# A decoder layer's up projection: the first two column pairs as plain products, the combinations of X on VectorE, and another order of the loads of h

## The chip, the cores and the metric

The kernel runs on one core of a Trainium2 chip. The metric is the device time of one execution in microseconds (us); of several runs the median is given.

## What is computed

One step of a one-layer decoder on 1056 rows: 32 sample rows (8 sequences of 4) and 1024 prompt rows, each 1024 wide. Attention, retention, their merge and the output projection come first. The change concerns what follows them, the convolutional feed-forward part, cut from the reference:

```
def conv_ffn(xn, conv_ctx, w_up, conv_w, conv_b, w_down):
    T = xn.shape[1]
    u = xn @ w_up
    u_ext = jnp.concatenate([conv_ctx.astype(u.dtype), u], axis=1)
    c = conv_b
    for tap in range(CONV_W):
        c = c + u_ext[:, tap:tap + T] * conv_w[tap]
    a, b = jnp.split(c, 2, axis=-1)
    h = jax.nn.gelu(a, approximate=True) * b
    return h @ w_down, u_ext[:, -(CONV_W - 1):]
```

w_up is 1024 x 6144, w_down 3072 x 1024. All values are float32.

## The kernel before, in words

**Precision.** Every float32 operand is kept as two parts, hi and lo. A product takes three matmuls: hi by hi, hi of the weight by lo of X, lo of the weight by hi of X (`mm3`, lines 238, 239, 240). `split` makes the parts: ScalarE casts hi (line 215), and `ew` subtracts it from the source to get lo, on VectorE (line 210) or GpSimd (line 212), as its first argument says. `V`, `G`, `S` and `TE` are VectorE, GpSimd, ScalarE and TensorE.

**Layout.** X, the normed input of the feed-forward part, lies transposed: 8 chunks of 128 features by 1056 columns (rows of the step). The columns are cut into four quarters of HW = 264, called (j, half): j = 0, 1 and half = 0, 1. A matmul here is 128 x 128 weights by 128 x 264 columns.

**Pairs.** w_up is worked through in 24 pairs of one gate block and one linear block of 128 columns each. A plain pair takes 8 chunk products for each of 2 blocks and 4 quarters, 192 matmuls: that is `eight`, used for pair 0. The other pairs use `pair(i)`, a Strassen-like scheme with seven products (A11, A12, A22, S1 to S4) instead of eight for each j, 168 matmuls. It needs sums of the four 128x512 parts of the weights (`up_weights`, on GpSimd), their hi and lo (`w_split`), and sums of quarters of X: `combos(j, ...)` makes t0, t1 and t2, `extra` splits three of them into the tiles ex40, ex50, ex20 (j = 0) and ex41, ex51, ex21 (j = 1), which serve the products S2, S3 and A22, and `t1` with `to_b12` writes one combination over a quarter of X itself. These combinations are made once and then serve all pairs. Part of this work is on GpSimd: the `ew(G, ...)` in `combos`, two instructions in `extra` (lines 911 and 912), and `t1(0, tmp, G)`.

**Pair 1 before.** It has an order of products of its own (`head`): A11, A12, S2, S3, S1, A22, S4. Its results are added to each other on VectorE as they come (lines 990 to 1012; line 1003 adds S1's, 998 and 999 add A11's to those of S2 and S3 in the usual order).

**Convolution and h.** After each pair, `conv` makes three taps on ScalarE and VectorE (lines 1052 to 1056), the gelu (1059), the product of both halves (a `ew` on c_out), and stores that block of h to HBM from GpSimd's queue (line 1062).

**Loads of h.** The down projection reads h back as two hi and lo parts. `load_h(0, n, ...)` loads n = 0 to 11 for j = 0: q = n % 6 takes four blocks of h (three for q = 5 at j = 0, whose fourth comes from SBUF), n // 6 is the half. So n = 5 and n = 11 need the h of pair 22, the others that of earlier pairs. The loads are issued during the last pair, two after each product, in the order 0 to 11, from GpSimd's queue (line 1035), into three buffers (`hrp`); each is then split into a place that the last pair no longer needs. For j = 0, n odd and below 6 the lo part is made on GpSimd. TensorE's first run through the down projection takes them in the order (0, q = 0 to 4), (1, q = 0 to 3), (0, 5), (1, 4), (1, 5), written (half, q), that is n = 0 to 4, 6 to 9, 5, 10, 11; each is 12 matmuls.

**What sets the order.** The code gives data and engines; the framework's scheduler places the instructions of each engine in a fixed order by its own model. So instructions of one pair, the conv of the one before and the combinations interleave, and an instruction waits for those in front of it on its engine even where its own data is ready.

Of the kernel before, what the change touches and what calls it, by code (L numbers as in the profile page):

```python
# [8 lines left out]
F32 = mybir.dt.float32  # L9
# [8 lines left out]
P = 128  # L18
# [6 lines left out]
T = NS + SEQ  # L25
# [94 lines left out]
def trunk(ctx, tc, I, O):  # L120
# [691 lines left out]
    def quad(j, r, half, a, b):  # L812
        c = (2 * j + half) * HW
        return [f32(x)[:, 4 * r:4 * r + 4, c + a:c + b] for x in X]

    def combos(j, a, b):
        b11, b12, b21, b22 = (quad(j, r, half, a, b) for r in range(2) for half in range(2))
        if j not in raws:
            raws[j] = [tr.tile([P, 4, HW], F32, name="t%d" % q) for q in range(3)]
        t2, t3, t = [x[:, :, a:b] for x in raws[j]]  # L820
        ew(V, t3, b22[0], b12[0], sub)
        ew(G, t, b22[1], b12[1], sub)
        ew(V, t3, t3, t, add)
# [83 lines left out]
    def extra(j, a, b):  # L907

        t2, t3, t = [x[:, :, a:b] for x in raws[j]]
        b21 = quad(j, 1, 0, a, b)  # L910
        G.tensor_tensor(out=t, in0=b21[0], in1=t2, op=sub)
        G.tensor_tensor(out=t, in0=t, in1=b21[1], op=add)
        for p, src in ((S2, t2), (S3, t3), (A22, t)):
            split(ex[p, j][:, 0, :, a:b], ex[p, j][:, 1, :, a:b], src)

# [48 lines left out]
    def pair(i):  # L964

        ws = up_weights(i)
        u, us = u_tile(i)
        banks, u3s, ts = {}, {}, {}
        head = i == 1

        def bank(j, b):
            if (j, b) not in banks:
                banks[j, b] = ps_8(j)
            return banks[j, b][:, :HW]

        def product(p, j, t):
            b, first = {A11: (0, True), A12: (0, False), S2: (1, True), S3: (1, False),
                        S1: (2, True), S4: (2, False), A22: (3, True)}[p]
            ps = bank(j, b)
            for k in range(4):  # L980
                xh, xl = xop(p, j, k)
                mm3(ps, t[:, k], t[:, 4 + k], xh, xl, first and k == 0, k == 3,
                    skip_group_check=not first)
            c12, c22 = u_dst(u, 0, j, 1), u_dst(u, 1, j, 1)
            if p == S3:
                u3s[j] = u3p.tile([P, HW], F32, name="u3")
            if p == A11 and head:
                S.copy(out=c22, in_=ps)
            elif p == S2 and head:
                V.tensor_tensor(out=c12, in0=ps, in1=c22, op=add)  # L990
            elif p == S3 and head:
                V.tensor_tensor(out=u3s[j], in0=ps, in1=c22, op=add)
            elif p == S2:
# [12 lines left out]
            if p == (A22 if head else A11):
                ps, u3 = bank(j, 3), u3s[j]
                if j == 0:
                    V.tensor_tensor(out=us[:, 1, :, 2:6], in0=smp(ps[:, :NS]), in1=smp(u3[:, :NS]),
                                    op=add)  # L1010
                    ps, u3 = ps[:, NS:], u3[:, NS:]
                V.tensor_tensor(out=u_dst(u, 1, j, 0), in0=ps, in1=u3, op=add)

        for p in (A11, A12, S2, S3, S1, A22, S4) if head else (S2, A22, S3, A11, S1, A12, S4):
            t = w_split(ws[p], G if p in (S3, A12) and not head else V)
            for j in range(2):
                product(p, j, t)
            if i == NPAIR - 1:
                hs.extend([load_h(0, len(hs) + e, slot(p, e)) for e in range(2 if p != S4 else 0)])
        return u, us  # L1020


# [7 lines left out]
    def load_h(j, n, sl):  # L1030

        q, c = n % 6, (2 * j + n // 6) * HW
        nk = 3 if j == 0 and q == 5 else 4
        raw = hrp.tile([P, 4, HW], F32, name="h_raw")[:, :nk]
        HL.dma_start(out=raw, in_=h_d[4 * q:4 * q + nk, :, c:c + HW].rearrange("k p c -> p k c"))
        put_h(sl, slice(0, nk), raw, G if HG(j, n) else V)
        return sl

    def put_h(sl, ks, src, eng=None):
# [26 lines left out]
    tmp = fup.tile([P, 2, UW], F32, name="u_ext").rearrange("p g x -> p (g x)")[:, :4 * HW]
    tmp = tmp.rearrange("p (k x) -> p k x", k=4)
    u, us = u_tile(0)
    wp = [wcols(w_up, g * NPAIR * P, P) for g in range(2)]

    def eight(j):
        for half in range(2):
            for g in range(2):
                ps = gemm_chunk(wp[g], actX, (2 * j + half) * HW, HW, ps=ps_8())
                evict(u, us, g, j, half, ps)

    eight(0)
    extra(0, 0, HW)
    t1(0, tmp, G)
    to_b12(0, tmp)  # L1080
    eight(1)
    combos(1, 0, J1B)
    combos(1, J1B, HW)
    extra(1, 0, HW)
    t1(1, raws[1][1], V)
    to_b12(1, raws[1][1])
    tr_stack.close()
    fp = pool("fp", 1, stack=fr_stack)
    hrp = pool("hrp", 3, stack=fr_stack)
    hs, HL = [], st  # L1090

    def HG(j, n):
        return j == 0 and n < 6 and n % 2 == 1

    conv(0, u, us)
    for i in range(1, NPAIR):
        u, us = pair(i)
        hlast = conv(i, u, us)
    for n in (5, 11):
# [41 lines left out]
    for j in range(2):  # L1141
        facc, nxt = [], []
        for m in range(KD):
            f = fd.tile([P, 2 * HW], F32, name="facc%d" % m)
            facc.append(f)
            last = m == KD - 1
            wts = [wcols(w_down, m * P, P, q3 * D) for q3 in range(3)]
            if j == 0 and m == 0:
                runs = [(0, q) for q in range(5)] + [(1, q) for q in range(4)] + [(0, 5), (1, 4), (1, 5)]
            elif m == 0 or last:  # L1150
                runs = [(half, q) for half in range(2) for q in range(6)]
            else:
                runs = [(half, 2 * q3 + e) for q3 in range(3) for half in range(2) for e in range(2)]
            pss = [ps_8()[:, :HW] for half in range(2)]
            if last and j == 1:
                break
            for n, (half, q) in enumerate(runs):
                wh, wl = wts[q // 2]
                for k in range(4):
                    hh, hl = (t[:, k] for t in hs[6 * half + q])  # L1160
                    kk = 4 * (q % 2) + k
                    mm3(pss[half], wh[:, kk], wl[:, kk], hh, hl, q == 0 and k == 0, q == 5 and k == 3)
                if q == 5:
                    S.copy(out=f[:, half * HW:half * HW + HW], in_=pss[half])
                if last:
                    if n < 6:
                        nxt.append(load_h(1, n, hs[n]))
                    elif n < 8:
                        nxt.append(load_h(1, n, FREE[n - 6]))
                        FREE.append(hs[n])  # L1170
                    else:
                        FREE.append(hs[n])
                        nxt.append(load_h(1, n, FREE[n - 6]))
        if j == 0:
            for r0, n in DROWS:
                final(0, r0, n)
            hs = nxt
    for half, c, w, rws in DLAST:
        ps = pss[0] if half == 0 else ps_8()[:, :w]
        for q in range(6):  # L1180
# [65 lines left out]
```

## Time and profile before

| what | value |
|---|---|
| median of 3 runs | 1760.26 us (1759.06 to 1760.69) |
| the profiled execution, its own time | 1756.41 us |
| its span, first to last instruction | 1754.6 us |
| TensorE busy | 1712.9 us (98%) |
| VectorE, ScalarE, GpSimd busy | 1081.6, 699.8, 455.5 us |
| mean granted TensorE clock | 0.995 |
| first matmul of the up projection, of the last pair | at 931.01, at 1418.82 us of the span |

The span is shorter than the execution's own time, since it counts from the first to the last instruction. A matmul's row shows some 0.28 us, though the next begins 0.12 us after it: they overlap in the pipeline, so the distance of their starts is their price. PE is TensorE, DVE VectorE, ACT ScalarE, POOL GpSimd; PEclk is the granted clock as a share of full speed.

### The profile page before, as it was taken

To read this page: it belongs to the slowest core of one execution; us is meant where nothing else is said; L and a number is where in the kernel's file an instruction comes from. 1 tells how busy PE (TensorE), PEld (TensorE's weight loads), DVE (VectorE), ACT (ScalarE), POOL (GpSimd) and SP (SyncE) were. 2 spreads that over 40 slices of the span, in tenths; PEclk is the share of its full clock that TensorE was granted. 3 is DMA by queue.
4 is the path that set the end of the run, shared out by engine and by line. 5 is a ranking of instruction groups with operands and counts; after the bars stand their busy time and mean duration, and the time that the engine had idled before them with its cause. 6 is when DMAs were issued, how large, how long until landed. Compare 5 with 4: busy or idle time off the path is not lost.

```text
span 1754.6 us, 31005 instructions
## 1 busy us (share of the span) xinstructions
PE 1712.9 (98%) x12513; PEld 1680.3 (96%) x12513; DVE 1081.6 (62%) x2084; ACT 699.8 (40%) x1464; POOL 455.5 (26%) x575
## 2 busy tenths in 40 slices
PE   6999999999999999999999899999999999999997
PEld 6999999999999999999789799999999999999997
DVE  6889654438484846545457987777777784127213
ACT  5544433224242435513324545444454553225222
POOL 4111111001111111000135765555545561003001
PEclk9999999999999999999999999999999999999999
DMA  8223234622222232443321122323222246338332
GB/s 226 62 80 94 70 115 145 209 73 62 91 63 89 64 106 71 172 133 100 102 85 66 50 90 88 96 73 95 89 74 74 82 144 209 97 95 273 105 97 76
DMA packets 196064, 183.60 MB, mean 105 GB/s; under 512 B 16208, under 2 KB 173552, under 8 KB 195904
## 3 DMA queue, kind: packets, MB, share of 16 engines
q1 hardware_dynamic: 180320, 128.46, 24.6%
q0 software_dynamic: 15600, 53.15, 8.6%
q8 instruction: 98, 1.61, 0.4%
q14 instruction: 46, 0.38, 0.1%
HBM read 137.87 MB, written 43.68 MB: 103 GB/s over the span
## 4 chain that ended last, share of the span: by engine, by line
PE 82%; issue 9%; DVE 4%; DMA 2%; POOL 1%; ACT 1%; SPq 1%; POOLq 0%; DVEq 0%; ACTq 0%
PE ps_mm L238 12%; PE ps_mm L239 12%; PE ps_mm L240 12%; PE ps_m L240 8%; PE ps_m L238 8%; PE ps_m L239 8%; PE ps_t L238 4%; PE ps_t L240 4%; PE ps_t L239 4%; DMA h_raw<-h_d 1%; PE ps_a L446 1%; PE ps_c L481 1%; DVE ex L210 1%; PE ps_b L469 1%; DVE t L210 0%
## 5 line engine op out<-in xcount | busy, mean ns | idle before, releaser
L238 PE MATMUL ps_mm<-xh,w_hi 128*128 128x384 f32 (+1 forms) x1080 | 354.7, 329 | 0.0
L239 PE MATMUL ps_mm<-xl,w_hi 128*128 128x384 f32 (+1 forms) x1080 | 352.9, 327 | 0.8 <-DVE xl L210 0.8
L240 PE MATMUL ps_mm<-xh,w_lo 128*128 128x384 f32 (+1 forms) x1080 | 351.5, 326 | 0.0
L210 DVE SCALAR_TENSOR_TENSOR w_lo<-w_raw,w_hi 128x1024 fp32r<-128x1024 f32 x107 | 130.7, 1222 | 231.2 <-ACT w_hi L229 231.0
L229 ACT CAST w_hi<-w_raw 128x1024 fp32r<-128x1024 f32 x108 | 113.3, 1049 | 282.4 <-PE ps_m L239 134.9
L239 PEld LDWEIGHTS ps_mm<-xl,w_hi 128*128 128x128 f32 x1080 | 204.0, 189 | 1.9 <-DVE xl L210 1.1
L238 PEld LDWEIGHTS ps_mm<-xh,w_hi 128*128 128x128 f32 x1080 | 204.1, 189 | 1.3 <-issue 1.0
L240 PEld LDWEIGHTS ps_mm<-xh,w_lo 128*128 128x128 f32 x1080 | 204.0, 189 | 0.7 <-issue 0.7
L1056 DVE SCALAR_TENSOR_TENSOR c_out<-u_ext,fconst,c_out 128x1024 f32<-128x1024 f32 x96 | 129.4, 1349 | 38.1 <-ACT c_out L1052 37.9
L265 POOL TENSOR_TENSOR rs<-ms,mhalf 128x1 f32<-128x1 f32 (+2 forms) x73 | 50.8, 697 | 367.9 <-DVE ms L263 255.1
L238 PE MATMUL ps_m<-xh,w_hi 128*128 128x264 f32 (+2 forms) x472 | 134.8, 286 | 2.7 <-ACT xh L215 2.7
L239 PE MATMUL ps_m<-xl,w_hi 128*128 128x264 f32 (+2 forms) x472 | 135.1, 287 | 0.7 <-DVE xl L210 0.6
L240 PE MATMUL ps_m<-xh,w_lo 128*128 128x264 f32 (+2 forms) x472 | 134.6, 285 | 0.0
L238 PE MATMUL ps_m<-xh,w 128*128 128x264 f32 x368 | 105.6, 287 | 8.8 <-DVE u_ext L1003 6.5
L238 PE MATMUL ps_m<-ex,w_hi 128*128 128x264 f32 x384 | 109.1, 284 | 0.9 <-ACT w_hi L229 0.9
L240 PE MATMUL ps_m<-ex,w_lo 128*128 128x264 f32 x384 | 109.4, 285 | 0.5 <-DVE w_lo L210 0.5
L239 PE MATMUL ps_m<-ex,w_hi 128*128 128x264 f32 x384 | 108.8, 283 | 0.0
L238 PE MATMUL ps_t<-xh,w 128*128 128x264 f32 x368 | 104.9, 285 | 0.8 <-DVE u_ext L1003 0.4
L240 PE MATMUL ps_m<-xh,w 128*128 128x264 f32 x368 | 105.2, 286 | 0.0
L239 PE MATMUL ps_m<-xl,w 128*128 128x264 f32 x368 | 105.1, 286 | 0.0
L239 PE MATMUL ps_t<-xl,w 128*128 128x264 f32 x368 | 104.7, 284 | 0.0
L240 PE MATMUL ps_t<-xh,w 128*128 128x264 f32 x368 | 104.3, 283 | 0.0
(384 smaller groups left out, 4903.6 us busy)
## 6 DMA issues: line engine op xcount, KB each, us to landing
w_raw<-in_w_up SPq DMA_DIRECT2D x48, 512.0 KB, 3.9
w_raw<-in_w_down SPq DMA_DIRECT2D x48, 512.0 KB, 3.9
w_raw<-in_w_in SPq DMA_DIRECT2D x42, 512.0 KB, 4.0
h_d<-c_out POOLq DMA_DIRECT2D x24, 528.0 KB, 3.0
h_raw<-h_d POOLq DMA_DIRECT2D x22, 528.0 KB, 5.2
xt<-in_x_prompt SPq DMA_DIRECT2D x16, 512.0 KB, 4.4
gm_d<-gstage POOLq DMA_DIRECT2D x22, 192.0 KB, 2.2
gm<-gm_d SPq DMA_DIRECT2D x8, 528.0 KB, 4.1
```

The costliest lines, as they stand in the source:

```text
L210: V.scalar_tensor_tensor(out=out, in0=in0, scalar=1.0, in1=in1, op0=mult, op1=op)
L229: S.copy(out=hi, in_=raw)
L238: TE.matmul(ps, wh, xh, start=start, stop=False, **kw)
L239: TE.matmul(ps, wh, xl, start=False, stop=False, **kw)
L240: TE.matmul(ps, wl, xh, start=False, stop=stop, **kw)
L265: G.tensor_tensor(out=rs[:r, :c], in0=ms[:r, :c], in1=mhalf[:r, :c], op=ALU.pow)
L446: TE.matmul(ps[:, jj, :], q, kS[s][v][:, kc], start=s == 0, stop=s == 1)
L469: TE.transpose(pt[:, h * P:(h + 1) * P], ph[:, s, h, :], identr)
L481: TE.matmul(po[:, v], w, pr[:, s, 2 * v:2 * v + 2, :], start=i == 0 and s == 0, stop=i == len(ops) - 1 and s == 1)
L1056: V.scalar_tensor_tensor(out=c[:, NS:], in0=u[:, g, NU + t:NU + t + SEQ], scalar=sc[t], in1=c[:, NS:], op0=mult, op1=add)
```

## The change

Pair 1 becomes a plain pair like pair 0; the special order of pair 1 goes. Every combination of X is made on VectorE, the one of A21 now inside `combos`. The place of t0, t1 and t2 is kept to the end, and the loads of h use these three buffers in turn instead of `hrp`. The loads are issued in the order 0, 1, 2, 3, 4, 6, 7, 8, 9, 10, 5, 11, and all their lo parts are made on VectorE. The scratch tile `tmp` becomes a c_out tile instead of a u_ext tile.

```diff
@@ combos(j, a, b)
         ew(V, t3, b22[0], b12[0], sub)
-        ew(G, t, b22[1], b12[1], sub)
+        ew(V, t, b22[1], b12[1], sub)
         ew(V, t3, t3, t, add)
         ew(V, t2, t3, b11[0], add)
         ew(V, t2, t2, b11[1], add)
+        ew(V, t, b21[0], t2, sub)
+        ew(V, t, t, b21[1], add)
@@ extra(j, a, b)
-        b21 = quad(j, 1, 0, a, b)
-        G.tensor_tensor(out=t, in0=b21[0], in1=t2, op=sub)
-        G.tensor_tensor(out=t, in0=t, in1=b21[1], op=add)
@@ pair(i)
-        head = i == 1
...
-        for p in (A11, A12, S2, S3, S1, A22, S4) if head else (S2, A22, S3, A11, S1, A12, S4):
-            t = w_split(ws[p], G if p in (S3, A12) and not head else V)
+        for p in (S2, A22, S3, A11, S1, A12, S4):
+            t = w_split(ws[p], G if p in (S3, A12) else V)
             for j in range(2):
                 product(p, j, t)
             if i == NPAIR - 1:
-                hs.extend([load_h(0, len(hs) + e, slot(p, e)) for e in range(2 if p != S4 else 0)])
+                for e, n in enumerate(LOADS.get(p, ())):
+                    hs[n] = load_h(0, n, slot(p, e))
@@ load_h(j, n, sl)
-        raw = hrp.tile([P, 4, HW], F32, name="h_raw")[:, :nk]
+        raw = tr.tile([P, 4, HW], F32, name="t%d" % (NRAW[0] % 3))[:, :nk]
+        NRAW[0] += 1
...
-        put_h(sl, slice(0, nk), raw, G if HG(j, n) else V)
+        put_h(sl, slice(0, nk), raw)
@@ the up projection
-    eight(0)
+    plain = [eight(0)]
     extra(0, 0, HW)
-    t1(0, tmp, G)
-    to_b12(0, tmp)
-    eight(1)
+    tmp = fp.tile([P, T], F32, name="c_out", bufs=3).rearrange("p (k x) -> p k x", k=4)
+    t1(0, tmp, V)
     combos(1, 0, J1B)
     combos(1, J1B, HW)
+    plain.append(eight(1))
     extra(1, 0, HW)
     t1(1, raws[1][1], V)
+    to_b12(0, tmp)
     to_b12(1, raws[1][1])
-    tr_stack.close()
...
+    LOADS = {S2: (0, 1), A22: (2, 3), S3: (4, 6), A11: (7, 8), S1: (9, 10), A12: (5, 11)}
...
-    conv(0, u, us)
-    for i in range(1, NPAIR):
+    for i, (u, us) in enumerate(plain):
+        conv(i, u, us)
+    for i in range(len(plain), NPAIR):
```

Before the change `eight(j)` did one half of pair 0; now `eight(i)` does the whole of pair i.

How the change moves instructions, at three places. In these rows the number after a tile's name only tells one instance from another.

GpSimd at the start of the up projection, before (u_ext_10160 is the scratch tile, t2 a combination, s0 to s3 the sums of weights):

```order
L212 TENSOR_TENSOR u_ext_10160<-xh_107,t0_9780 128x1056
L901 TENSOR_TENSOR s0_10455<-w_raw_10453 128x512
L903 TENSOR_TENSOR s2_10457<-w_raw_10451,w_raw_10453 128x512
L212 TENSOR_TENSOR u_ext_10160<-u_ext_10160,xl_108 128x1056
L955 COPY u_ext_10161<-fconst_10157 128x8x2 x2
L902 TENSOR_TENSOR s1_10456<-s0_10455,w_raw_10451 128x512
L212 TENSOR_TENSOR t2_10401<-xl_108 128x4x136
L212 TENSOR_TENSOR t2_10401<-xl_108 128x4x128
```

and after it, the same stretch:

```order
L952 MEMSET u_ext_10165 128x2x2
L952 MEMSET u_ext_10417 128x2x2
L954 COPY u_ext_10165<-fconst_10159 128x8x2 x2
L954 COPY u_ext_10417<-fconst_10159 128x8x2 x2
L1039 COPY fconst_10159<-u_ext_10165 128x16 x2
L1037 COPY fconst_10159<-u_ext_10165 128x2x2
L1039 COPY fconst_10159<-u_ext_10417 128x16
L903 TENSOR_TENSOR s0_10699<-w_raw_10697 128x512
L905 TENSOR_TENSOR s2_10701<-w_raw_10695,w_raw_10697 128x512
L904 TENSOR_TENSOR s1_10700<-s0_10699,w_raw_10695 128x512
```

The combinations are gone from GpSimd, and the sums of pair 1's weights too; those of pair 2 come first.

VectorE around the end of the combinations for j = 1, before (line 1003 is the addition that pair 1's products wait for, w7 a split weight):

```order
L990 TENSOR_TENSOR u_ext_10463<-ps_m_10531,u_ext_10463 128x264
L210 SCALAR_TENSOR_TENSOR ex41_10154<-t0_10399,ex41_10154 128x1056
L210 SCALAR_TENSOR_TENSOR ex51_10155<-t1_10400,ex51_10155 128x1056
L210 SCALAR_TENSOR_TENSOR t1_10400<-xh_107,t0_10399 128x1056
L992 TENSOR_TENSOR u3_10574<-ps_m_10531,u_ext_10463 128x264
L210 SCALAR_TENSOR_TENSOR t1_10400<-t1_10400,xl_108 128x1056
L1003 TENSOR_TENSOR u_ext_10463<-ps_m_10593,u3_10574 128x264
```

and after, up to ex21:

```order
L210 SCALAR_TENSOR_TENSOR c_out_10666<-c_out_10666,c_out_10658 128x1056
L210 SCALAR_TENSOR_TENSOR ex41_10156<-t0_10400,ex41_10156 128x1056
L210 SCALAR_TENSOR_TENSOR t2_10402<-t2_10402,xl_108 128x4x136
L210 SCALAR_TENSOR_TENSOR ex51_10157<-t1_10401,ex51_10157 128x1056
L210 SCALAR_TENSOR_TENSOR t2_10402<-t2_10402,xl_108 128x4x128
L210 SCALAR_TENSOR_TENSOR xl_108<-c_out_10397,xh_107 128x4x264
L1048 SCALAR_TENSOR_TENSOR c_out_10678<-u_ext_10417,fconst_10159,c_out_10678 128x32
L210 SCALAR_TENSOR_TENSOR t1_10401<-xh_107,t0_10400 128x1056
L1048 SCALAR_TENSOR_TENSOR c_out_10686<-u_ext_10417,fconst_10159,c_out_10686 128x32
L210 SCALAR_TENSOR_TENSOR ex21_10158<-t2_10402,ex21_10158 128x1056
```

No addition of a pair's results stands among the combinations any more; the products that run meanwhile are plain, and ScalarE empties their banks.

GpSimd's queue in the last pair, before (the three-block loads, 128x3x264, are n = 5 and n = 11):

```order
L1062 DMA h_d_63<-c_out_16006 128x1056
L1045 COPY fconst_10157<-u_ext_16027 128x16 x2
L1035 DMA h_raw_16142<-h_d_63 128x3x264
L1035 DMA h_raw_16182<-h_d_63 128x4x264
L1035 DMA h_raw_16186<-h_d_63 128x4x264
L1102 DMA out_conv_sT<-fconst_10157 128x768
L1043 COPY fconst_10157<-u_ext_16027 128x2x2
L212 TENSOR_TENSOR ex51_10155<-h_raw_16142,ex51_10155 128x792
L1103 DMA out_conv_pT<-fconst_10157 128x96
L1035 DMA h_raw_16221<-h_d_63 128x4x264
```

and after:

```order
L1029 DMA t0_16175<-h_d_63 128x4x264
L1056 DMA h_d_63<-c_out_15999 128x1056
L1039 COPY fconst_10159<-u_ext_16020 128x16
L1029 DMA t1_16179<-h_d_63 128x4x264
L1039 COPY fconst_10159<-u_ext_16020 128x16
L1096 DMA out_conv_sT<-fconst_10159 128x768
L1029 DMA t2_16214<-h_d_63 128x4x264
L1029 DMA t0_16218<-h_d_63 128x4x264
L1029 DMA t1_16252<-h_d_63 128x3x264
L1037 COPY fconst_10159<-u_ext_16020 128x2x2
```

The store of pair 22's h was followed at once by the load that reads it; now n = 8, 9 and 10 stand between them.

## Rows read from the trace of the kernel before

**Rows 1.** The page: the chain that ended last, by engine
```profile
PE 82%; issue 9%; DVE 4%; DMA 2%; POOL 1%; ACT 1%; SPq 1%; POOLq 0%; DVEq 0%; ACTq 0%
```

**Rows 2.** Windows, TensorE: stretch, length, busy (records), granted clock, DMA share, GB/s
```profile
931.00:951.62 20.62, 20.62 (x173) 1.00 0.15 51
931.00:1051.62 120.62, 111.15 (x881) 0.97 0.21 67
1051.62:1418.82 367.20, 367.20 (x3026) 1.00 0.26 84
1418.82:1477.18 58.36, 53.71 (x411) 0.94 0.72 224
...
850.00:931.00 81.00, 81.00 (x381) 1.00 0.23 82
```

**Rows 3.** Waits of TensorE in the whole span: us in total, times, longest
```profile
PE ps_m L238 <- DVE u_ext L1003: 6.5, 1, 6.5
PE ps_m L238 <- ACT xh L215: 2.7, 1, 2.7
PE ps_m L238 <- DVE u L999: 2.3, 3, 1.3
...
PE ps_t L239 <- DVE ex L210: 0.8, 1, 0.8
```

**Rows 4.** Timeline of VectorE, start of the up projection: start, us, instruction
```profile
899.52 1.25 DVE L210 SCALAR_TENSOR_TENSOR t<-xh 128x1056 f32<-128x1056 f32 x1
...
970.97 2.20 DVE L210 SCALAR_TENSOR_TENSOR t<-xh,t 128x1056 f32<-128x1056 f32 x1
...
973.44 3.27 DVE L210 SCALAR_TENSOR_TENSOR t<-t,xl 128x1056 f32<-128x1056 f32 x1
```

**Rows 5.** Timeline of GpSimd, the same stretch
```profile
973.18 2.40 POOL L912 TENSOR_TENSOR t<-t,xl 128x1056 f32<-128x1056 f32 x1
...
983.00 1.29 POOL L212 TENSOR_TENSOR w<-s,w 128x512 fp32r<-128x512 f32 x1 [2.30 <-ACT w L889]
```

**Rows 6.** Windows, all engines: PE, PEld, DVE, ACT, POOL busy, then as rows 2
```profile
977.00:980.00 3.00, 2.90 (x13) 2.90 (x14) 2.56 (x6) 2.31 (x3) 3.00 (x3) 0.50 0.10 25
...
967.00:979.00 12.00, 4.71 (x29) 4.28 (x29) 11.96 (x11) 3.24 (x7) 12.00 (x8) 0.82 0.00 0
...
1442.00:1457.00 15.00, 11.64 (x88) 10.89 (x87) 10.86 (x11) 6.95 (x8) 6.46 (x8) 0.97 1.06 348
...
1457.00:1460.00 3.00, 3.00 (x15) 3.00 (x15) 1.71 (x3) 2.02 (x2) 0.64 (x1) 0.50 0.94 334
```

**Rows 7.** Timeline of GpSimd in the last pair; a DMA row is its issue
```profile
1430.32 2.78 POOL L212 TENSOR_TENSOR ex<-h_raw,ex 128x1056 fp32r<-128x1056 f32 x1 [2.46 <-ACT ex L215]
1434.51 0.57 POOL L1062 DMA_DIRECT2D h_d<-c_out  x1 [1.42 <-DVE c_out L210]
...
1438.73 2.27 POOL L1035 DMA_DIRECT2D h_raw<-h_d  x3 [0.85 <-DMA h_d<-c_out]
...
1446.59 0.76 POOL L1035 DMA_DIRECT2D h_raw<-h_d  x1
```

**Rows 8.** The tile h_raw, and a piece of the chain from 1442 to 1457
```profile
L215 ACT CAST xh<-h_raw x12: 844/1072/1082, 1446.3 to 1600.0; 128x1056 fp32r<-128x1056 f32 x11, 128x792 fp32r<-128x792 f32 x1
...
DMA to landing us min/median/max: 4.0/4.9/8.5
...
1446.59 7.60 DMA h_raw<-h_d
```

**Rows 9.** Timeline of VectorE in the last pair
```profile
1430.69 3.52 DVE L210 SCALAR_TENSOR_TENSOR c_out<-c_out 128x1056 f32<-128x1056 f32 x1
...
1434.48 0.42 DVE L999 TENSOR_TENSOR u<-ps_m,u 128x264 f32<-128x264 f32 x1
```

**Rows 10.** Timelines of GpSimd, VectorE and TensorE in pair 22, before A12 of j = 1
```profile
1405.68 1.29 POOL L901 TENSOR_TENSOR s<-w_raw 128x512 f32<-128x512 f32 x1 [4.50 <-DMA w_raw<-in_w_up]
...
1413.72 0.42 DVE L999 TENSOR_TENSOR u<-ps_t,u 128x264 f32<-128x264 f32 x1
...
1414.44 0.28 PE L238 MATMUL ps_t<-xh,w 128*128 128x264 f32 x1
```

More of the change, by code (lines that the diff above doesn't have):

```diff
@@ L967, in pair @@
         u, us = u_tile(i)
-        banks, u3s, ts = {}, {}, {}
-        head = i == 1
+        banks, u3s = {}, {}
         def bank(j, b):
@@ L986, in product @@
                 u3s[j] = u3p.tile([P, HW], F32, name="u3")
[L987 to L993, printed above, removed]
+            if p == S2:
                 S.copy(out=c12, in_=ps)
@@ L1005, in product @@
                 V.tensor_tensor(out=c12, in0=ps, in1=c12, op=add)
-            if p == (A22 if head else A11):
+            if p == A11:
                 ps, u3 = bank(j, 3), u3s[j]
@@ L1063, in conv, with eight @@
         return cs[1]
[L1066 to L1075, printed above, removed]
-    eight(0)
+    fp = pool("fp", 1, stack=fr_stack)
+    def eight(i):
+        u, us = u_tile(i)
+        wp = [wcols(w_up, (g * NPAIR + i) * P, P) for g in range(2)]
+        for j in range(2):
+            for half in range(2):
+                for g in range(2):
+                    ps = gemm_chunk(wp[g], actX, (2 * j + half) * HW, HW, ps=ps_8(j))
+                    evict(u, us, g, j, half, ps)
+        return u, us
+    plain = [eight(0)]
     extra(0, 0, HW)
-    t1(0, tmp, G)
-    to_b12(0, tmp)
-    eight(1)
+    tmp = fp.tile([P, T], F32, name="c_out", bufs=3).rearrange("p (k x) -> p k x", k=4)
+    t1(0, tmp, V)
     combos(1, 0, J1B)
     combos(1, J1B, HW)
+    plain.append(eight(1))
     extra(1, 0, HW)
     t1(1, raws[1][1], V)
+    to_b12(0, tmp)
     to_b12(1, raws[1][1])
-    tr_stack.close()
[L1088 to L1093, printed above, removed]
-    conv(0, u, us)
-    for i in range(1, NPAIR):
+    hs, HL, NRAW = {}, st, [0]
+    LOADS = {S2: (0, 1), A22: (2, 3), S3: (4, 6), A11: (7, 8), S1: (9, 10), A12: (5, 11)}
+    for i, (u, us) in enumerate(plain):
+        conv(i, u, us)
+    for i in range(len(plain), NPAIR):
         u, us = pair(i)
@@ L1176, in trunk @@
                 final(0, r0, n)
-            hs = nxt
+            hs = dict(enumerate(nxt))
     for half, c, w, rws in DLAST:
@@ L1190, in trunk @@
     fr_stack.close()
+    tr_stack.close()
     e_stack.close()
```

## Prediction

> **What bounds the kernel now.** I read the chain that ended last first: TensorE's own work is 82% of it [rows 1]. So time can only be won where TensorE stands still, and the view by windows says where. From the first to the last ordinary pair, TensorE is busy 367.20 of 367.20 us [rows 2]: 18 pairs of 168 matmuls, 3024 in all, so one matmul of 128x264 costs 367.20 / 3024 = 0.1214 us when nothing is in the way. That is my ruler. The first window of that group holds 157 matmuls and 16 transposes; 157 x 0.1214 = 19.06 leaves 1.6 us for the transposes.
>
> *Start of the up projection, 931.00 to 1051.62.* It holds pair 0 (192 matmuls) and four pairs (672): 864 x 0.1214 + 1.6 = 106.5 us of work in 120.6 us [rows 2]. **14.1 us are lost here.** Half is one wait of 6.5 us for VectorE's line 1003 [rows 3]. What VectorE did in that time: two instructions on 1056 columns of t, 2.20 and 3.27 us, stood in front of the 1003 that TensorE wanted, where a like one earlier took 1.25 us [rows 4]. GpSimd meanwhile ran the sums of pair 2's weights and the A21 combination, 2.40 us for its second step; a GpSimd instruction of 512 columns took 1.29 at 983.00 [rows 5]. Both were busy for 11.96 and 12.00 of 12 us [rows 6]. After the wait the granted clock was 0.50, the lower of the two levels, and matmuls stood 2.90 / 13 = 0.22 us apart [rows 6]: some 18 of them, 1.8 us more. The remaining 5 to 6 us are small waits in the first pairs, for an ex tile 0.8 and two of the three for line 999 [rows 3] among them.
>
> *The tail, 1418.82 to 1477.18.* The last pair (168) and the first 240 matmuls of the down projection are 408 x 0.1214 = 49.5 us of work in 58.4 us [rows 2]. **8.8 us are lost.** On GpSimd's queue the load of n = 5 wants the h of pair 22, whose store goes out at 1434.51; so n = 5 waits until 1438.73, n = 6 and 7 behind it, and n = 8 goes out at 1446.59 [rows 7]. These loads land after a median of 4.9 and at most 8.5 us, the one of 1446.59 after 7.60 [rows 8]. The DMA engines' share is 1.06, full, from 1442 to 1457 [rows 6]. TensorE waits 2.7 us for a cast of such a load [rows 3], then runs at a granted clock of 0.50 again [rows 6], 26 matmuls at 0.22 us, 2.6 us. Before that it loses 1.3 of the 2.3 us put down to line 999 [rows 3]: VectorE spent 3.52 us in one product of c_out beside a GpSimd split of 2.78 us [rows 7], and reached 999 at 1434.48 only [rows 9].
>
> **The change, part by part.**
>
> *Pair 1 as eight products.* 192 matmuls for 168: 24 x 0.1214 = **+2.9 us**, all on the path. It takes away the special order of pair 1, whose first product already needed the combinations. Now TensorE has 384 matmuls, 46.6 us, plus 1.6 of transposes that need nothing but X and two weight blocks, until 979.3. The low half of pair 1's weights is split on VectorE after the seventh group has left its buffer: 931.0 + 7 x 2.91 + 1.6 = 953.0, then a cast and a split of about 1.25 us [rows 4] with a like instruction or two in front, some 957. TensorE asks for it about 959. I cost it at nothing; without that cover it would be one wait of the 2 to 3 us that those instructions take.
>
> *Combinations on VectorE alone.* From ex40 to ex21 its order holds seven combination steps in two halves each, four convolution steps, nine splits, sums and products of 1056 columns and one w_lo: 21 x 1.25 = 26 us [rows 4], with the small ones and the halving about 30, from 946 on, so to 976 if undisturbed. GpSimd still makes the four sums of pair 2's weights; at 1.29 each in VectorE's way that is 981. ex41 stands early in that order, ready near 972, wanted at 981; ex21 is wanted at 983.9. So the waits of the start should go: **-14.1 us**. VectorE's instructions are no cheaper than GpSimd's for that; they run under 384 matmuls that don't need them, instead of during pair 1, which did. In the stage before, the w_o products, VectorE takes three more instructions of 1.25 us. TensorE waits for nothing there, 81.00 of 81.00 us busy [rows 2], and the GpSimd instructions that stretched VectorE's go; I cost it at nothing, and if all three were exposed it would be 3.8.
>
> *What is late next.* Pair 2's weight sums start when VectorE is fullest. In the ordinary rhythm GpSimd's first sum waits for its weights until 1405.68, and the addition on which A12 depends ends at 1413.72 + 0.42 = 1414.14, where TensorE wants it at 1414.44 [rows 10]: 0.3 us of slack. Pair 2's A12 conversion comes 2 us later in its pair than that. Bounds: 0.3 us (one late A12, the rest absorbed) to 4 us (the five small waits of the first pairs as before). I take **+1.5 us**, nearer the lower, because pair 2 now starts with all of its data-side combinations ready.
>
> *Loads in the new order, splits on VectorE.* The two loads that need pair 22 (n = 5 and 11) go last; n = 8 goes out near 1437 instead of 1446.6, since nothing ahead waits for a store (I let the loads follow each other by the 2.3 us of a cast and a split). GpSimd's splits (2.78) become VectorE's (1.25), which shortens what stood ahead of 999. This takes the **-8.8 us**. The three load buffers were there before; now they are t0 to t2, so no wait is added. What is late next are n = 5, out near 1445.3, and n = 11, near 1450: with 4.9 to land, 1.07 to cast [rows 8] and 1.25 to split they are ready at 1452.5 and 1457.2, where TensorE reaches them 108 and 132 matmuls after the last pair ends at 1439.2, at 1452.3 and 1455.3. Bounds: 0.5 us, and with the longest landing of 8.5 [rows 8] 1460.8 - 1455.3 = 5.5 us. I take **+2.0**, near what the median gives.
>
> **Sum:** -14.1 + 2.9 + 1.5 - 8.8 + 2.0 = -16.5 us. The profiled execution took 1756.41 us, so 1739.9; the median of the runs, 1760.26, is 3.85 above it, so **1743.8 us**. With the bounds of the two estimated terms this case alone spans -19.2 to -10.5, 1741 to 1749.8.
>
> **Rivals.**
>
> *The tail stays bound by landing times* (0.15). The DMA engines are full there [rows 6], and moving requests forward does not make bytes: n = 8 took 7.60 us although little stood ahead of it [rows 8]. If every load lands in 7 to 8.5, TensorE catches up with them and loses its clock again: the tail gains nothing, -14.1 + 2.9 + 1.5 = -9.7, so 1750.6. Against it: at an issue 6 to 10 us earlier, most loads fall outside the crowded stretch.
>
> *VectorE becomes the bound of the start* (0.11). It was full for 12 us [rows 6], and all the work of GpSimd is given to it. If each of eight GpSimd instructions left there holds it by 3.27 - 1.25 = 2.0 us [rows 4], its 30 us become 46, ex21 is ready at 992 and TensorE stands for 8 us and loses 1.8 at the lower clock: +10. With the tail's -6.8 that is -14.1 + 2.9 + 1.5 + 10 - 6.8 = -6.5, so 1753.8. For it: the rows of the collisions. Against it: fewer GpSimd instructions are left to collide with. The Trainium skill, Perfetto Trace Analysis, section Optimizing Scalar/DVE Operations, speaks against the change: a saturated VectorE is relieved by handing work to ScalarE or even GpSimd. The same section adds that these two share a read port, so that it might not help, and the trace agrees with that addition: 2.20 and 3.27 us beside GpSimd, 1.25 without.
>
> *Both waits only move* (0.03): start and tail each get back all but a few us, 1757 to 1763.
>
> *Slower: pair 2's lateness is handed on* (0.03). An A12 conversion that is late delays the release of the weight buffer, the next load, the next sums and the next A12; with 0.3 us of slack [rows 10] it could repeat in all 21 later pairs. From 16.5 / 21 = 0.8 us in each pair the change loses; at 1.5 us in each it costs 21 x 1.5 = 31.5, less the 16.5 (with the 1.5 counted once): +13.5, 1773.8. Against it: the kernel before entered its pairs late as well, and from 1051.62 on lost nothing [rows 2].
>
> That the change does not do what it says is ruled out by the order of GpSimd and VectorE; what remains is timing.
>
> **Numbers.** 0.68 for the forecast. The range of 1740 to 1754 takes in its bounds, the first rival and about half of the second. About 0.2%, 3.5 us, is what a measurement of this kernel can tell from no change. Faster by more than that (below 1756.7): 0.68 + 0.15 and most of the second, together 0.90; within it 0.06, slower 0.04.
>
> **What would show it.** The wait for 1003 is gone from TensorE's list; the first Strassen-like pair starts near 979, and the one that starts at 1051.62 now near 1042; the granted clock shows no 0.50 at either place; n = 8 goes out near 1437; the longest wait in the tail is for n = 5 or n = 11, below 3 us. A wait over 5 us around 981 for an ex tile would show the second rival, small waits at every 20.40 us up to 1418 the slower one, landings of 7 us at n = 5 to 10 with a lower clock the first. A start still over 117 us long, or a last pair's tail over 56, would make the prediction wrong in its main terms.

## The result, and the profile after

| | before | changed |
|---|---|---|
| median | 1759.93 us (6 runs, 1755.04 to 1762.08) | 1745.13 us (6 runs, 1743.87 to 1748.29) |
| ratio | | 0.9923, 95% interval 0.9907 to 0.9939 |
| span of the profiled execution | 1754.6 us | 1743.4 us |

The change makes the kernel faster by 0.8%, 13.5 us by the ratio (10.7 to 16.4). Of TensorE's windows in the changed kernel (columns as in [rows 2]) the first is the stretch to pair 5, the second pair 2, the third pairs 5 to 22, the fourth the tail:

```profile
931.88:1047.13 115.25, 111.45 (x906) 0.99 0.23 71
980.29:1006.32 26.03, 22.23 (x170) 0.93 0.19 62
1047.13:1414.33 367.20, 367.20 (x3027) 1.00 0.26 83
1414.33:1463.89 49.56, 49.56 (x410) 1.00 0.82 252
```

Against [rows 2], the start takes 115.25 us instead of 120.62 (-5.4), the pairs behind it the same 367.20, the last pair and 240 matmuls of the down projection 49.56 instead of 58.36 (-8.8). 49.56 is 408 x 0.1214: the tail has no loss left. The sum, -14.2, is more than the spans differ by, since this execution reached the up projection 0.9 us later (931.88 against 931.01; 931.0 to 933.4 in all 14 profiles) and needed 2.1 us more after the tail, 1.7 of them after TensorE's last instruction. The change moves three instructions of the stage before the up projection to VectorE and gives the loads of h other buffers to the end; whether it has a part in either isn't shown (after TensorE's last instruction the 14 profiles need 9.0 to 12.1 us).

The waits of TensorE in the changed kernel, where [rows 3] had 6.5 for line 1003, 2.7 for a cast and 2.3 for 999 (now line 991):

```profile
PE ps_t L238 <- DVE u L991: 2.5, 1, 2.5
...
PE ps_m L238 <- DVE u L991: 1.3, 1, 1.3
```

Both are in pair 2, the only pair longer than 20.40 us. What stands before them on VectorE (timeline; the columns as in [rows 4]):

```profile
972.80 1.25 DVE L210 SCALAR_TENSOR_TENSOR ex<-t,ex 128x1056 fp32r<-128x1056 f32 x1
...
979.04 1.25 DVE L210 SCALAR_TENSOR_TENSOR ex<-t,ex 128x1056 fp32r<-128x1056 f32 x1
980.21 1.28 DVE L1048 SCALAR_TENSOR_TENSOR c_out<-u_ext,fconst,c_out 128x32 f32<-128x32 f32 x1
...
982.58 0.24 DVE L1048 SCALAR_TENSOR_TENSOR c_out<-u_ext,fconst,c_out 128x32 f32<-128x32 f32 x1
...
985.70 2.32 DVE L1050 SCALAR_TENSOR_TENSOR c_out<-u_ext,fconst,c_out 128x1024 f32<-128x1024 f32 x1
...
988.54 1.27 DVE L1050 SCALAR_TENSOR_TENSOR c_out<-u_ext,fconst,c_out 128x1024 f32<-128x1024 f32 x1
989.74 0.68 DVE L210 SCALAR_TENSOR_TENSOR w<-s,w 128x512 fp32r<-128x512 f32 x1
...
991.72 2.16 DVE L210 SCALAR_TENSOR_TENSOR c_out<-c_out 128x1056 f32<-128x1056 f32 x1
993.80 1.77 DVE L210 SCALAR_TENSOR_TENSOR w<-w_raw,w 128x512 fp32r<-128x512 f32 x1
...
995.83 0.42 DVE L991 TENSOR_TENSOR u<-ps_m,u 128x264 f32<-128x264 f32 x1
997.38 2.01 DVE L210 SCALAR_TENSOR_TENSOR w<-s,w 128x512 fp32r<-128x512 f32 x1 [1.13 <-ACT w L891]
...
1000.06 0.41 DVE L991 TENSOR_TENSOR u<-ps_t,u 128x264 f32<-128x264 f32 x1
```

The first two rows are ex41 and ex21: they are in time. But behind ex21 come another 15 us of VectorE's work before pair 2's first 991, and windows of all engines (columns as in [rows 6]) show that VectorE had no gap to make it up:

```profile
948.00:997.00 49.00, 47.71 (x393) 47.50 (x392) 47.59 (x51) 27.59 (x47) 25.63 (x21) 1.00 0.14 45
...
981.00:997.00 16.00, 14.71 (x121) 14.50 (x120) 15.15 (x15) 7.13 (x13) 10.13 (x10) 1.00 0.13 37
```

Not all of that is VectorE's own work. Four rows before the first 991 take longer than like ones: 1.28 us instead of 0.24 (980.21), 2.32 instead of 1.27 (985.70), 2.16 instead of 1.25 (991.72), 1.77 instead of 0.68 (993.80), 4.1 us in all, and GpSimd was at work beside each of them. TensorE's wait for that 991 (995.83) is the shorter one, 1.3 us. Before the longer one, for the 991 at 1000.06, VectorE did have a gap: the split at 997.38 stands in front of that 991, waited 1.13 us for a cast, and then took 2.01 us instead of 0.68. The cast in turn had waited for one of GpSimd's sums of pair 3's weights:

```profile
996.73 1.14 ACT L891 CAST w<-s 128x512 fp32r<-128x512 f32 x2 [5.21 <-POOL s L904]
```

In the tail, GpSimd's queue (timeline, as in [rows 7]; load issues stand on line 1029 now) and VectorE's product of c_out that the store waits for:

```profile
1427.54 0.56 POOL L1056 DMA_DIRECT2D h_d<-c_out  x1 [1.10 <-DVE c_out L210]
...
1438.93 0.75 POOL L1029 DMA_DIRECT2D t<-h_d  x1 [2.59 <-DVE c_out L1048]
...
1444.95 0.74 POOL L1029 DMA_DIRECT2D t<-h_d  x1 [2.39 <-DVE xl L210]
```

```profile
1425.99 1.25 DVE L210 SCALAR_TENSOR_TENSOR c_out<-c_out 128x1056 f32<-128x1056 f32 x1
```

That product took 3.52 us before [rows 9]. The store of pair 22 goes out 13.2 us after the last pair's first matmul instead of 15.7 [rows 7], n = 5 (1438.93) 24.6 instead of 19.9, n = 11 (1444.95) 30.6. No load is waited for.

### The profile page after: what moved, and what is told of

It reads as the page before. It is cut to its first block, busy times and chain, and to the rows that moved or that the text cites. A ratio compares the mean times of both kernels' runs of the same rounds, so it can differ in the third digit from the quotient of the medians.

```text
span 1743.4 us, 31027 instructions
## 1 busy us (share of the span) xinstructions
PE 1709.9 (98%) x12537; PEld 1680.0 (96%) x12537; DVE 1071.1 (61%) x2082; ACT 698.5 (40%) x1464; POOL 410.8 (24%) x559
## 4 chain that ended last, share of the span: by engine, by line
PE 83%; issue 7%; DVE 4%; DMA 3%; POOL 1%; ACT 1%; POOLq 0%; SPq 0%; DVEq 0%; ACTq 0%
PE ps_mm L239 13%; PE ps_mm L238 13%; PE ps_mm L240 13%; PE ps_m L240 8%; PE ps_m L239 8%; PE ps_m L238 8%; PE ps_t L238 4%; PE ps_t L240 4%; PE ps_t L239 4%; DMA t<-h_d 1%; PE ps_a L446 1%; PE ps_c L481 1%; DMA g_pre<-in_g_pre_mix 1%; PE ps_b L469 1%; DVE t L210 0%
## 5 line engine op out<-in xcount | busy, mean ns | idle before, releaser
L1050 DVE SCALAR_TENSOR_TENSOR c_out<-u_ext,fconst,c_out 128x1024 f32<-128x1024 f32 x96 | 125.1, 1303 | 39.6 <-ACT c_out L1046 39.5
L265 POOL TENSOR_TENSOR rs<-ms,mhalf 128x1 f32<-128x1 f32 (+2 forms) x73 | 47.1, 646 | 379.0 <-DVE ms L263 372.8
L240 PE MATMUL ps_m<-ex,w_lo 128*128 128x264 f32 (+1 forms) x388 | 110.3, 285 | 0.6 <-DVE w_lo L210 0.6
L238 PE MATMUL ps_m<-ex,w_hi 128*128 128x264 f32 (+1 forms) x388 | 109.8, 284 | 0.0
L239 PE MATMUL ps_m<-ex,w_hi 128*128 128x264 f32 (+1 forms) x388 | 109.7, 283 | 0.0
L238 PE MATMUL ps_t<-xh,w 128*128 128x264 f32 x352 | 100.7, 286 | 2.5 <-DVE u L991 2.5
L238 PE MATMUL ps_m<-xh,w 128*128 128x264 f32 x352 | 100.2, 285 | 1.3 <-DVE u L991 1.3
L239 PE MATMUL ps_t<-xl,w 128*128 128x264 f32 x352 | 100.7, 286 | 0.0
L240 PE MATMUL ps_t<-xh,w 128*128 128x264 f32 x352 | 100.3, 285 | 0.0
L240 PE MATMUL ps_m<-xh,w 128*128 128x264 f32 x352 | 100.1, 284 | 0.0
L239 PE MATMUL ps_m<-xl,w 128*128 128x264 f32 x352 | 100.0, 284 | 0.0
```

The costliest lines, as they stand in the source:

```text
L238: TE.matmul(ps, wh, xh, start=start, stop=False, **kw)
L239: TE.matmul(ps, wh, xl, start=False, stop=False, **kw)
L240: TE.matmul(ps, wl, xh, start=False, stop=stop, **kw)
L265: G.tensor_tensor(out=rs[:r, :c], in0=ms[:r, :c], in1=mhalf[:r, :c], op=ALU.pow)
L1050: V.scalar_tensor_tensor(out=c[:, NS:], in0=u[:, g, NU + t:NU + t + SEQ], scalar=sc[t], in1=c[:, NS:], op0=mult, op1=add)
```

## The experiments

Twelve kernels, all with a profile. "Start" is from the first matmul of the up projection to the first of pair 5. "Tail" is the loss: from the last pair's first matmul to the first transposition of an output, less the number of matmuls between (1320 in most) times 0.1214 (more exactly 367.20 / 3024). Each ratio is to runs of the kernel before that were made together with that kernel's; their medians are 1757.88 to 1760.51, so kernels are better compared by ratio than by median.

| run | start | tail loss | median | ratio to before (interval) |
|---|---|---|---|---|
| before | 120.6 | 8.7 | 1759.93 | 1 |
| changed | 115.3 | 0.3 | 1745.13 | 0.9923 (0.9907 to 0.9939) |
| start_only | 114.0 | 9.0 | 1754.99 | 0.9983 (0.9974 to 0.9993) |
| tail_only | 120.9 | 0.3 | 1750.56 | 0.9956 (0.9942 to 0.9971) |
| old_order | 114.0 | 0.8 | 1747.55 | 0.9941 (0.9926 to 0.9956) |
| g_splits | 113.9 | 8.0 | 1755.58 | 0.9981 (0.9971 to 0.9992) |
| g13 | 113.9 | 5.9 | 1751.86 | 0.9960 (0.9948 to 0.9972) |
| g5 | 115.2 | 0.9 | 1745.43 | 0.9922 (0.9909 to 0.9936) |
| sp_loads | 115.5 | 9.0 | 1755.09 | one run |
| g13_copy | 113.8 | 5.3 | 1749.64 | 0.9947 (0.9932 to 0.9962) |
| head_v | 121.4 | 0.3 | 1750.38 | 0.9948 (0.9934 to 0.9961) |
| g_combos | 118.1 | 0.3 | 1746.80 | 0.9924 (0.9907 to 0.9940) |
| a12_first | 115.1 | 0.3 | 1746.45 | 0.9927 (0.9915 to 0.9940) |
| b12_v | 117.1 | 0.3 | 1747.32 | 0.9935 (0.9923 to 0.9948) |

Among the kernels with the two waits of pair 2 as above, starts of 114 and of 115 differ by TensorE's clock (last section).

**Are there two separate gains?** start_only, from the changed kernel:

```diff
-    LOADS = {S2: (0, 1), A22: (2, 3), S3: (4, 6), A11: (7, 8), S1: (9, 10), A12: (5, 11)}
+    LOADS = {S2: (0, 1), A22: (2, 3), S3: (4, 5), A11: (6, 7), S1: (8, 9), A12: (10, 11)}
-        put_h(sl, slice(0, nk), raw)
+        put_h(sl, slice(0, nk), raw, G if j == 0 and n < 6 and n % 2 == 1 else V)
```

> The changed kernel with the tail as before: loads of h in the order 0 to 11 and the lo parts of n = 1, 3, 5 on GpSimd. Theory A (two separate gains: some 5.4 us net at the start, 8.8 us in the tail): the start as in the changed kernel (115.3 us from the first matmul of the up projection to the first of pair 5), the tail (last pair and 240 matmuls) back near 58.4 us, so about 5 us under the kernel before, near 1754. Rival B (the tail gains because VectorE and GpSimd no longer collide early in the up projection and h is stored earlier): the tail stays below 53 us, and the time near 1748.

tail_only, from the kernel before:

```diff
-                hs.extend([load_h(0, len(hs) + e, slot(p, e)) for e in range(2 if p != S4 else 0)])
+                for e, n in enumerate(LOADS.get(p, ())):
+                    hs[n] = load_h(0, n, slot(p, e))
-        put_h(sl, slice(0, nk), raw, G if HG(j, n) else V)
+        put_h(sl, slice(0, nk), raw)
```

> The kernel before with the new order of loads and all lo parts on VectorE, everything else (head order of pair 1, combinations on GpSimd, hrp buffers) as before. Theory A: the start as before, 120.6 us to pair 5; the tail 49.6 us, with no wait; about 8.8 us under the kernel before, near 1751. Rival B: the tail keeps half or more of its loss, over 54 us, and the time is above 1755.

In the windows both came out as theory A has it. In start_only the tail is back at a loss of 9, in tail_only it is at none:

```profile
931.72:1045.73 114.01, 110.15 (x905) 1.00 0.23 73
1413.10:1471.69 58.59, 52.67 (x411) 0.94 0.69 216
```

```profile
933.23:1054.08 120.85, 111.37 (x882) 0.97 0.21 67
1421.28:1470.84 49.56, 49.56 (x410) 1.00 0.83 255
```

In time, tail_only gains 7.7 us by its ratio (5.1 to 10.2) and start_only 3.0 (1.2 to 4.6), less than the 5.4 of theory A, though its start is 6.6 us shorter. In its profile some 4 us are lost again behind the tail (281.4 us from the tail's end to the end of the span, before 277.5); no run shows why.

**What makes the tail's gain: the order of loads or the engine of the lo parts?** old_order puts only the first line of start_only's diff back, g_splits only the second.

> The changed kernel with only the order of the loads put back to 0 to 11; all lo parts stay on VectorE. Theory A (the order makes the gain, since the load that waits for the store of pair 22 holds up those behind it): n = 6 to 10 go out some 8 us later, TensorE waits 2 to 4 us for a cast of a load and its clock falls, tail 55 to 58 us, time 5 to 8 us above the changed kernel. Rival C (the lo parts on VectorE make the gain): tail below 52 us, time within 2 us of the changed kernel.

> The changed kernel with only the lo parts of n = 1 and 3 (the odd ones below 6 and n = 5) put back on GpSimd; the new order of loads stays. Theory A: the 1.5 us wait for line 999 in the last pair comes back (line 991 here) and little else: tail 50 to 52 us, time 0.5 to 2.5 us above the changed kernel. Rival C: tail above 54 us, time 5 us or more above the changed kernel.

Theory A falls here, on both. With the old order the tail still loses only 0.8 us in the profiled execution; with GpSimd's three lo parts and the new order it loses 8.0. TensorE in g_splits waits as it did before the change:

```profile
PE ps_m L238 <- ACT xh L215: 3.2, 1, 3.2
```

and in old_order the tail's 408 matmuls need 50.52 us, with one wait of 0.7:

```profile
1413.40:1463.92 50.52, 49.79 (x411) 1.00 0.82 253
```

In old_order the load of n = 5 still goes out some 4 us behind the store of pair 22 (1430.91 after 1426.65; before, 1438.73 after 1434.51 [rows 7]). But the store goes out 13.2 us into the last pair, as in the changed kernel, and so n = 5 goes out 17.5 us into it instead of 19.9. The time says less than the tail: old_order's median is 2.4 us above the changed kernel's, by the ratios 3.2, with intervals that overlap, and two of its four runs are near 1750. What the order is worth in those isn't shown.

**Which of the three lo parts, and by what way?**

```diff
+        put_h(sl, slice(0, nk), raw, G if j == 0 and n in (1, 3) else V)      (g13)
+        put_h(sl, slice(0, nk), raw, G if j == 0 and n == 5 else V)           (g5)
-    hs, HL, NRAW = {}, st, [0]                                  (sp_loads, from start_only)
+    hs, HL, NRAW = {}, ld, [0]
```

> The changed kernel with the lo parts of n = 1 and 3 on GpSimd, n = 5 on VectorE. The tail of the last four runs depends on the engine of the lo parts (8.0 and 9.0 us lost with three of them on GpSimd, 0.3 and 0.8 with none), not on the order of the loads. Theory D (two early splits hold up VectorE and the loads that stand behind them in GpSimd's queue, and everything after runs late): the tail loses 5 to 8 us as with all three, time near 1754. Rival E (the late one, n = 5, is what TensorE waits for, 1.9 us on GpSimd and last in line): the tail loses under 2 us, time near 1748.

> The changed kernel with only the lo part of n = 5 on GpSimd. Theory D: the tail loses 1 to 2 us, what a split of 1.9 us takes more than one of 1.0, time 1 to 2 us above the changed kernel. Rival E: it loses 5 us or more, time near 1752.

> The old tail (order 0 to 11, three lo parts on GpSimd) in the changed kernel, but the loads of h go out from SyncE's queue, where the splits don't stand in front of them. Theory D1 (the loss comes from the loads that wait behind a split in GpSimd's queue): n = 4 goes out some 1.3 us earlier and the tail loses under 4 us instead of 9.0. Theory D2 (the loss comes from the engines' collisions and the later buffers): it still loses 7 us or more. The loads of w_down share that queue, so waits for w_hi can come in both.

The two early ones cost 5.9 of the 8.0, the late one 0.9 (0.6 over the changed kernel): theory D by the tail, while g13's time, 1751.86, lies between the two forecasts, 1754 and 1748. sp_loads still loses 9.0, so a split in front of the loads in GpSimd's queue is not the main way. It is a weak run, though, since those loads then stand among the loads of w_down, and only one was timed. In g13 the two splits on GpSimd

```profile
1418.95 2.46 POOL L212 TENSOR_TENSOR ex<-t,ex 128x1056 fp32r<-128x1056 f32 x1
...
1425.34 2.49 POOL L212 TENSOR_TENSOR ex<-t,ex 128x1056 fp32r<-128x1056 f32 x1
...
1439.46 3.46 POOL L1037 COPY fconst<-u_ext 128x4 f32<-128x4 f32 x1 [0.56 <-DVE u_ext L997]
...
1443.76 1.50 POOL L1029 DMA_DIRECT2D t<-h_d  x2
```

stand beside these two rows of VectorE:

```profile
1417.67 4.83 DVE L1050 SCALAR_TENSOR_TENSOR c_out<-u_ext,fconst,c_out 128x1024 f32<-128x1024 f32 x2
...
1426.13 2.80 DVE L210 SCALAR_TENSOR_TENSOR w_lo<-w_raw,w_hi 128x1024 fp32r<-128x1024 f32 x1
```

Two convolution steps take 4.83 us instead of the changed kernel's 2.56, a w_lo 2.80 instead of 1.22: 3.9 us that VectorE loses in the last pair, where it works from 1416.49 to 1444.07 almost without a gap. The 2.49 us of GpSimd also stand ahead of the store. The last two GpSimd rows suggested one more way, a small copy in front of the load of n = 5, which g13_copy takes out:

```diff
-        G.tensor_copy(out=cpr[:, :, :, i].rearrange("p w g -> p g w"), in_=u[:, :, UW - 2:UW])
+        cp = S.copy if i == NPAIR - 1 else G.tensor_copy
+        cp(out=cpr[:, :, :, i].rearrange("p w g -> p g w"), in_=u[:, :, UW - 2:UW])
```

> The run with the lo parts of n = 1 and 3 on GpSimd, in which one more thing is moved: pair 23's copy of four columns into fconst goes from GpSimd to ScalarE. In that run this copy stood in front of the load of n = 5 for 3.46 us beside VectorE, and n = 5 went out at 1443.8 instead of 1438.9. Theory H (that queue position is the larger part): n = 5 goes out 3 us or more earlier and the tail loses under 3 us instead of 5.9. Rival D (VectorE's stretched steps and late buffers are): the tail still loses 5 us or more.

The load of n = 5 goes out 27.8 us into the last pair (1440.54) instead of 30.3, and the tail still loses 5.3: rival D holds, the copy is worth 0.6. How the rest divides between VectorE's stretched steps and the later release of buffers wasn't separated.

**What makes the start's gain?** head_v lets pair 1 run in its special order again (the lines of `pair` before, and no `eight(1)`); g_combos puts the combinations back:

```diff
-        ew(V, t, b22[1], b12[1], sub)
+        ew(G, t, b22[1], b12[1], sub)
-        ew(V, t, b21[0], t2, sub)
-        ew(V, t, t, b21[1], add)
+        ew(G, t, b21[0], t2, sub)
+        ew(G, t, t, b21[1], add)
-    t1(0, tmp, V)
+    t1(0, tmp, G)
```

> The changed kernel with pair 1 again in its special order of seven products (168 matmuls), all combinations staying on VectorE. Theory A (the start is won because 384 matmuls run before the combinations are needed): TensorE waits again for a combination in pair 1, 5 us or more in all, and the first matmul of the up projection to the first of pair 5 takes 118 to 125 us instead of 114 to 115; time 4 to 10 us above the changed kernel. Rival G (it is won by taking GpSimd out of VectorE's way): the start takes below 114 us, since 24 matmuls less are to be done, time at or below the changed kernel.

> The changed kernel with pair 1 plain, but the combinations of before (b22 - b12 of lo, the two of A21, t1 of j = 0) on GpSimd again. Theory A: they are hidden under the 384 matmuls as well, the start takes 114 to 118 us, time within 3 us of the changed kernel; pair 2's two waits stay or grow by 1 to 2 us, since GpSimd starts the sums later. Rival G: TensorE waits 3 us or more before or at the start of pair 2, the start takes 119 us or more.

VectorE alone gains nothing: with the special order the start takes 121.4 us, and TensorE waits 4.9 us in pair 1, for a weight's cast and an ex tile (3.2 and 1.7; the wait of 1.9 is in pair 3):

```profile
932.58:1053.96 121.38, 113.88 (x882) 0.94 0.21 67
```

```profile
PE ps_m L238 <- ACT w L891: 3.2, 2, 2.4
PE ps_t L238 <- DVE u L998: 1.9, 1, 1.9
PE ps_t L239 <- DVE ex L210: 1.7, 1, 1.7
```

So the start's gain needs the plain pair. Whether it needs VectorE too stays open: g_combos' profiled start is 2.8 us longer (118.1, with 28.9 us in pair 2), but that execution was its longest of four (1750.02), and the ratios, 0.9924 and 0.9923, don't differ.

**What makes pair 2 long, and can it be had back?** In the changed kernel ScalarE's cast of the last combination (row 1) waits for VectorE and stands ahead of the cast of the A12 weights (row 2), GpSimd then converts them (row 3), and only then is the next weight block loaded, which GpSimd's sums (row 4) wait for:

```profile
982.74 1.07 ACT L215 CAST xh<-t 128x1056 fp32r<-128x1056 f32 x1 [2.44 <-DVE t L210]
983.72 0.62 ACT L891 CAST w<-w_raw 128x512 fp32r<-128x512 f32 x1
...
984.42 2.51 POOL L212 TENSOR_TENSOR w<-w_raw,w 128x512 fp32r<-128x512 f32 x1 [2.98 <-ACT w L891]
...
990.95 1.81 POOL L903 TENSOR_TENSOR s<-w_raw 128x512 f32<-128x512 f32 x1 [2.88 <-DMA w_raw<-in_w_up]
```

a12_first casts and splits A12 ahead of that; b12_v lets VectorE write the hi part of the last combination:

```diff
+    early = {2: (up_weights(2), {p: w_tile() for p in (S2, A22, S3, A11, S1, A12)})}
+    w_split(early[2][0][A12], G, early[2][1][A12])                            (a12_first)
     to_b12(0, tmp)
-    to_b12(1, raws[1][1])                                                     (b12_v, with t1's lines)
+    ew(V, hi, out, b22[1], add)
+    ew(V, out, out, b22[1], add)
+    ew(V, lo, out, f32(hi), sub)
```

> The changed kernel with pair 2's A12 weights cast and split ahead of the cast of the last combination (both engines and all amounts of work unchanged, only their order). In the changed kernel that cast on ScalarE (982.74) waits for VectorE's last step and stands in front of A12's cast (983.72), GpSimd then converts until 986.9, and only then the weights of pair 3 are loaded. Theory A (this chain makes the two waits in pair 2): the second weight block's load starts some 3 us earlier, pair 2 lasts 20.4 to 22 us instead of 24.8 to 26.0, time 2.5 to 4.5 us under the changed kernel. Rival F (VectorE's own queue, full with convolution and combinations, makes them): pair 2 stays above 24 us, time within 1 us of the changed kernel.

> The changed kernel with one cast taken off ScalarE: VectorE writes the hi part of the last combination itself (one instruction of 1.25 us more), so that the cast of pair 2's A12 weights has no cast that waits for VectorE in front of it. Theory A2 (A12's conversion, and with it the load of pair 3's first block, is held by that cast): the load goes out 2.5 us or more earlier, pair 2 takes 20.4 to 22.5 us instead of 24.8 to 26.0, time 2.5 to 4.5 us under the changed kernel. Rival F (VectorE's queue is what is late): pair 2 stays above 24 us, time within 1 us of the changed kernel or above it.

Both theories fall: A12's conversion doesn't make the waits. In a12_first only A12 came early; another split of the same weight block moved behind the cast in its place, and pair 2 took 25.9 us. In b12_v the A12 conversion was done at 982.3 instead of 986.9, and pair 2 took 27.9:

```profile
981.04 1.30 POOL L212 TENSOR_TENSOR w<-w_raw,w 128x512 fp32r<-128x512 f32 x1
...
988.42 2.24 POOL L903 TENSOR_TENSOR s<-w_raw 128x512 f32<-128x512 f32 x1 [5.95 <-DVE w L210]
```

```profile
983.00:999.00 16.00, 11.66 (x97) 11.45 (x95) 15.89 (x14) 4.71 (x9) 10.50 (x8) 0.98 0.12 34
```

VectorE is busy for 15.89 of 16 us there, and TensorE's one wait is for a 991 behind them, 4.6 us: in b12_v VectorE's queue is what is late (rival F). But the added instruction of 1.24 us is the smaller part. GpSimd's sums started 2.5 us earlier than in the changed kernel, and four VectorE instructions beside them (989.44, 991.67, 993.37, 995.78) took 8.5 us where like ones take 4.5, two of them

```profile
993.37 2.31 DVE L1050 SCALAR_TENSOR_TENSOR c_out<-u_ext,fconst,c_out 128x1024 f32<-128x1024 f32 x1
995.78 2.14 DVE L210 SCALAR_TENSOR_TENSOR c_out<-c_out 128x1056 f32<-128x1056 f32 x1
```

The changed kernel's longer wait and a12_first's only one ended otherwise, behind a weight split for which VectorE stood idle (1.13 and 1.51 us) until GpSimd's sum and its cast had come, and which then took 2.01 and 3.04 us instead of 0.68. So pair 2's lateness comes through VectorE, but its own queue, GpSimd's sums beside it and the late sum weren't taken apart: no run only took work off VectorE there, and g_combos, which gave combinations back to GpSimd, has the longest pair 2. No kernel of these beats the changed one beyond the intervals.

## Why the prediction was right, and where it was not

The forecast was 1743.8 us, and 1745.13 came out. Step by step:

- **Pair 1 plain, -14.1 + 2.9: right.** The wait for 1003 is gone, no ex tile is waited for, the first Strassen-like pair starts 48.4 us after the first matmul (forecast 48.3), and w_lo was in time. ex41 was ready at 974.1 and ex21 at 980.3; I had 972, and 976 to 981. That VectorE alone wouldn't have done it is shown by head_v; that the plain pair alone does isn't shown (g_combos).
- **"What is late next", +1.5 with bounds 0.3 to 4: wrong in size and place.** Pair 2 lost 5.6 us (26.03 instead of 20.40; 4.4 where the clock held). The step that failed is the count of VectorE's work, which stopped at ex21. What TensorE needs next are pair 2's 990 and 991, and 15 us of convolution, the last combination, splits and weights stood before them, lengthened by 4.1 us beside GpSimd's instructions; the longer of the two waits came behind a split that waited for pair 3's sums. I looked for the lateness on GpSimd's conversion of A12; advancing that, in b12_v, made pair 2 longer.
- **The tail, -8.8: right, by half the reason.** The loss is gone entirely. I put it to the order of loads first and to the splits second; in the profiles the splits are worth 7.7 us (g_splits) to 8.2 (old_order against start_only) and the order 0.5 to 1.0. Pair 22's store goes out 2.5 us earlier, since VectorE's product before it is not stretched any more, and in the new order n = 5 goes out 11.4 us behind it, so no load waits for it.
- **"Late loads", +2.0: nothing.** n = 5 went out 1.9 us earlier into the last pair than I worked out, n = 11 0.6, and TensorE waited for neither.
- Errors of +4.3 us at the start and -2.0 in the tail are behind a sum that is off by 2.3 (-14.2 against -16.5). That the total came so near is in part luck: the two errors have opposite signs. The range held it.

Of the rivals, the one of landing times fell: the DMA share is 0.82 in the tail, and TensorE doesn't wait. Its long landings did come, 7.0 to 8.1 us for n = 9, 10 and 5, but TensorE wanted none of them before it was there. The one of VectorE as the bound of the start named the right engine and what holds it, GpSimd's instructions, at about half its price and in pair 2 rather than at its start. Lateness handed on from pair to pair didn't occur: from 1006.32 on every pair takes 20.40 us.

## What to carry to other kernels

When work moves onto an engine that has cover, count that engine's queue up to the next instruction that the bounding engine waits for, not to the last of the moved ones, and add what a neighbour engine stretches there. Two engines that slow each other cost time where one of them has no slack: two short splits on GpSimd in the last pair cost 6 us, though GpSimd was busy for only 24% of the span (g13). And take the two halves of an edit apart in separate runs before you credit the plausible one.

## What was not expected of the hardware

GpSimd's copy of four columns takes 0.19 us at the median of its 24 instances in the changed kernel. At 1439.46 in g13 it took 3.46, until three VectorE instructions without a gap between them (1439.32, 1440.48, 1441.62) had ended; so a short GpSimd instruction can be held through several of VectorE's. The Trainium skill, SBUF — State Buffer, section Summary: rules for kernel authors, has the later of two such instructions blocked until the other has finished, where VectorE's has two inputs from SBUF and GpSimd's reads SBUF. The stretched rows agree with that (4.83 instead of 2.56 for two steps beside a 2.46 us split); of a wait through more than one instruction it says nothing.

After the same 2.5 us wait in pair 2, TensorE was granted its full clock (2.4 GHz) in start_only and the lower one (1.2 GHz) in the changed kernel, whose code is the same up to there, so that it loses 1.2 us in one execution and not in another. old_order, g_splits and g13 went as start_only did, g5 and sp_loads as the changed kernel:

```profile
1000.40:1003.40 3.00, 2.96 (x24) 1.00 0.00 0
```

```profile
1000.50:1003.50 3.00, 2.97 (x13) 0.50 0.00 0
```
